# Pairing local kernels in one PSUM bank, holding a weight split back, and reordering two short tails in a decoder trunk

## The chip, the cores and the metric

The kernel runs on one core of one Trainium2 chip. The metric is the device time in microseconds (us); three runs of the kernel before gave 1273.04, 1273.29 and 1273.45 us, so 1273.29 us is its median. The five engines of the core are named as the profile names them: PE (matrix multiply; PEld is its weight load), DVE (vector), ACT (scalar and activation), POOL (GpSimd) and SP (which mostly issues DMAs). Each engine works through its own instructions in program order, and waits where one needs another engine's result.

## What is computed

Two layers with a width of 1024 over 256 tokens, in fp32. Each layer is a half-step SwiGLU feed-forward block (FFN), a mixer, a cross-attention into 256 memory tokens, and a second FFN, all with a residual add and an RMS norm in front. Layer 0 mixes with S5, a diagonal state-space model over 64 groups of 16 channels; layer 1 with RetNet retention. The end is one more RMS norm.

```python
def _rmsnorm(x, g):
    return x * lax.rsqrt(jnp.mean(x * x, axis=-1, keepdims=True) + EPS) * g

def reference(x, mem, ...):
    mem_n = _rmsnorm(mem, mem_norm)
    for i in range(DEPTH):
        g = norm_gains[i]
        x = x + 0.5 * _swiglu(_rmsnorm(x, g[0]), ffn1_w_in[i], ffn1_w_out[i])
        h = _rmsnorm(x, g[1])
        mix = _s5_mixer(h, ...) if i % 2 == 0 else _retention_mixer(h, positions, ...)
        x = x + mix
        x = x + _memory_cross_attention(_rmsnorm(x, g[2]), mem_n, ...)
        x = x + 0.5 * _swiglu(_rmsnorm(x, g[3]), ffn2_w_in[i], ffn2_w_out[i])
    return _rmsnorm(x, final_norm)

# S5: state x_t = a * x_{t-1} + Bbar u_t (complex, diagonal), then
y = gelu(real(C x_t) + d_skip * u);  a, gate = split(y @ w_glu);  mix = a * sigmoid(gate)
```

## The kernel before

**Precision and weights.** Every large product is made of three matmuls: both factors are split into a rounded part (`hi`) and the rest (`lo`), and hi·hi, hi·lo and lo·hi are summed in PSUM. `Stream` (`ws`, line 35) feeds the weights in the fixed order of `plan`: a DMA on SP's queue fills one of 5 `raw` buffers, ACT copies it to `wh` (line 87), DVE subtracts to `wl` (line 89, or line 106 where the subtraction was held and released), for at most 7 open pieces. Where in the program a split is issued is decided when the program is written out: `tick()` may split one piece, if a rough clock (`ws.t`) says that its DMA has landed, and `get()` forces the piece that is needed. `ws.limit` names the first piece in the plan that a tick must not split. A forced `get` does not look at it.

**Order.** The schedule is manual: engines run what the program text issues, in that order. `bg` is a list of background generators; the FFN and projection loops call `bg_step()` between their matmuls, and each call runs a generator to its next `yield`.

**The tables of S5** (`s5_tables`, line 576) are such a generator. It runs inside the first FFN, up to some 197 us. Its last loop goes over 8 index values `q` ("quarters" in the code). `vrev(q, part)` lets DVE make a reversed table in `Vr2`, which has two slots, `q % 2`; `vt(q, b)` transposes half of it on PE (4 transposes into a bank named `tp`), and ACT copies it out; `kernels(q)` (line 750) makes the local convolution kernel of 8 steps: 8 calls of `small` (matmuls with 32 columns of weights, 16 records in the trace), into 128 columns of a `tp` bank, one ACT copy to `pads`, and one short DVE operation that adds the skip term. `ca` makes another table on DVE.

**PSUM.** `acc()` takes one of 6 banks, `ptb()` one of 2. A pool gives out the bank that has been free the longest, counted along the program text. So which bank a tile gets depends on which tiles were released before it.

**The S5 input** (`S5In`, line 792; `s5`, line 824). After the first FFN the normalised input goes to DRAM (`xn_d`) and comes back re-laid as `xc`. Meanwhile `fill(us)` feeds PE with pieces of the memory's key and value projections: `kv_unit(0, u)` for units 0 to 5, 48 steps in all; one step is 6 matmuls of 128x256 for units 0 to 3 and of 128x512 for units 4 and 5. `fill(11.8)` (line 848) takes 19 steps: units 0 and 1 whole, each ending in a split of its bank by ACT (`kvh`) and DVE (`kvl`), and steps 0 to 2 of unit 2. Unit 2 has two weight pieces: `(("kv",0,2),0)` for steps 0 to 3 and `(("kv",0,2),1)` for steps 4 to 7. Then ACT and DVE copy `xc` to `xg`, two each in turn (line 852); PE transposes `xg` in 4 groups of 4 into the two `pt` banks, and ACT and DVE copy them to `U` (line 857); `fill(1.0)` takes steps 3 and 4 of unit 2; and the products `v` from `U` follow (line 868).

**The S5 output** (from line 938). After the scan over 32 chunk states (DVE, lines 887 to 890), `carry(q)` adds the carried state to the banks `ybank` with `small` matmuls; `gelu(0)` reads the banks of q 0 to 3 and `gelu(1)` those of q 4 to 7. `y_out(hf)` (line 942) transposes one time half of the result on PE, 2 times 4, into `pt` banks, and splits it into `yT` hi and lo. These splits have strided targets and are slow. `ws.hold()` keeps four subtractions of the output weights back until `ws.release()`, after the scan. `fill(1.3)` takes one step of unit 5. Then `glu_blocks` multiplies by the output weights, whose first block needs both halves: four matmuls with the weights that go with `y_out(0)`, then four with those of `y_out(1)`.

**The last norm** (`Final.stat`, line 1277) is called once per 128 tokens. The second call is the end of the program: ACT sums squares of both halves of the row (`mean_sq`, line 289), POOL adds them and EPS (line 282) and raises to -0.5 (line 283), DVE and ACT scale 512 columns each and each half goes out in its own DMA.

Of the kernel before, what the change touches and what calls it, by code (L numbers as in the profile page):

```python
# [10 lines left out]
F32 = mybir.dt.float32  # L11
# [3 lines left out]
AF = mybir.ActivationFunctionType  # L15
ALU = mybir.AluOpType
AX = mybir.AxisListType

P = 128
# [5 lines left out]
EPS = 1e-6  # L25
# [114 lines left out]
def tile_trunk(ctx: ExitStack, tc: tile.TileContext, I: dict, out: bass.AP):  # L140
    nc = tc.nc
    pe, act, dve, pool = nc.tensor, nc.scalar, nc.vector, nc.gpsimd
# [5 lines left out]
    sm = ctx.enter_context(tc.tile_pool(name="sm", bufs=2))  # L148
# [4 lines left out]
    def acc(name="acc"):  # L153
        return ps_acc.tile([P, 512], F32, tag="acc", name=name)

    def ptb(name="pt"):
        return ps_t.tile([P, 512], F32, tag="pt", name=name)
# [73 lines left out]
    ws = Stream(nc, raw_pool, w_pool, plan)  # L231
# [3 lines left out]
    neghalf = cpool.tile([P, 2], F32, tag="neghalf", name="neghalf")  # L235
    gT = cpool.tile([P, 72], F32, tag="gT", name="gT")
    x = big.tile([P, 2, D], F32, tag="x", name="x")
# [9 lines left out]
    def small(o, a, b, start, stop, at):  # L247
        ws.t += 0.074
        pe.matmul(o, lhsT=a, rhs=b, start=start, stop=stop, tile_position=at)  # L249
# [22 lines left out]
    rstd = {}  # L272
# [13 lines left out]
    def mean_sq(src, ss):  # L286

        junk = sm.tile([P, D], BF16, tag="junk", name="junk", bufs=1)
        act.activation(junk[:, 0:src.shape[-1]], src, AF.Square, scale=1.0 / 32.0, accum_out=ss)  # L289

    def ssq(src, parts=1):
        ss = sm.tile([P, 2], F32, tag="ss", name="ss", bufs=4)
        for i in range(parts):
            n = D // parts
            mean_sq(src[:, i * n:i * n + n], ss[:, i:i + 1])
        return rsqrt(ss[:, 0:1], 4, "rstd", ss[:, 1:2] if parts == 2 else None)
# [279 lines left out]
    def s5_tables():  # L576
# [15 lines left out]
        pt = ptb()  # L592
# [69 lines left out]
        for n in (1, 2, 4):  # L662
            t = [sm.tile([P, 4, 32], F32, tag="t512", name="tp", bufs=2)[:, 0:n] for _ in range(2)]
            a = [pw[:, c, n:n + 1].to_broadcast([P, n, 32]) for c in range(2)]
# [15 lines left out]
        t = [sm.tile([P, 32, 16], F32, tag="t512", name="tb", bufs=2) for _ in range(2)]  # L680
# [4 lines left out]
        E16 = sm.tile([P, 16], F32, tag="E16", name="E16", bufs=1)  # L685
        dve.tensor_reduce(E16, ident.rearrange("p (b h) -> p h b", h=16), axis=AX.X, op=ALU.add)
        dT = sm.tile([P, 8], F32, tag="dT", name="dT", bufs=1)
        pt = ptb()
# [6 lines left out]
        Cb = big.tile([P, 2, 32, 2, 16], F32, tag="W1", name="Cb")  # L695
        pool.memset(Cb.rearrange("p a b c d -> p (a b c d)"), 0.0)
        yield
        for c in range(2):
            for b in range(2):
                pt = acc("tp").rearrange("p (t r) -> p t r", t=4)  # L700
# [12 lines left out]
        Vr2 = big.tile([P, 2, 2, 4, 8, 16], F32, tag="Mh", name="Vr2")  # L713
# [27 lines left out]
        def vt(q, b):  # L741
            pt = acc("tp").rearrange("p (a e) -> p a e", a=4)
            for i in range(4):
                tr(pt[:, i], Vr2[:, q % 2, i % 2, 2 * b + i // 2].rearrange("p s h -> p (s h)"), ident)
            o = Yl[:, q] if q < 2 else sY[:, 0]
            act.copy(o[:, 512 * b:512 * b + 512], pt.rearrange("p a e -> p (a e)"))
            if b and q >= 2:
                pool.dma_start(out=tabV[q], in_=sY[:, 0])

        def kernels(q):  # L750
            Vr, pd = Vr2[:, q % 2], pads[q // 4][:, q % 4]
            pt = acc("tp")
            for c in range(2):
                for j in range(4):
                    small(pt[32 * j:32 * j + 32, 0:P], Cb[:, c, j * 8 + q].rearrange("p g h -> p (g h)"),
                          Vr[:, c, j].rearrange("p s h -> p (s h)"), c == 0, c == 1, (0, 32 * j))
            act.copy(pd, pt[:, 0:P].rearrange("p (s h) -> p s h", h=16))
            dve.scalar_tensor_tensor(out=pd[:, 7], in0=E16, scalar=dT[:, q:q + 1], in1=pd[:, 7], op0=ALU.mult, op1=ALU.add)

        for part in range(2):  # L760
            vrev(0, part)
            yield
        for q in range(8):
            vt(q, 0)
            if q < 7:
                vrev(q + 1, 0)
            yield
            vt(q, 1)
            kernels(q)
            if q < 7:  # L770
                vrev(q + 1, 1)
            yield
            for part in range(2):
                ca(q, part)
                yield
# [48 lines left out]
    def s5(si, kv, fill, nxt):  # L824
# [9 lines left out]
        def local_table(q):  # L834
# [6 lines left out]
            for b in range(2):  # L841
# [3 lines left out]
                    tr(pt[:, i], pd[:, 7 - t:15 - t].rearrange("p s h -> p (s h)"), ident)  # L845
                act.copy(lv[:, 4 * b:4 * b + 4], pt.rearrange("p t (g h) -> p t g h", h=16))

        fill(11.8)
        alt = [act.copy, dve.tensor_copy]
        xg = big.tile([P, 16, 8, 16], F32, tag="xTh", name="xg")  # L850
        for b in range(4):
            alt[b % 2](xg[:, 4 * b:4 * b + 4], si.xc[:, :, 64 * b:64 * b + 64].rearrange("p s (g h) -> p g s h", h=16))
        for b in range(4):
            pt = ptb().rearrange("p (g e) -> p g e", g=4)
            for i in range(4):
                tr(pt[:, i], xg[:, 4 * b + i].rearrange("p s h -> p (s h)"), ident.rearrange("p (t j c) -> p j t c", t=2, j=4))
            alt[b % 2](U[:, 4 * b:4 * b + 4], pt)
        fill(1.0)
        vc = big.tile([P, 8, 2, 2, 64], F32, tag="xTh", name="vc")
        for b in range(4):  # L860
            bank = acc("v").rearrange("p (q c g s) -> p q c g s", q=2, c=2, g=2)
            for ql in range(2):
                q = 2 * b + ql
                t = tv[q] if q < 4 else tab("tabV", q)
# [10 lines left out]
        for b in range(4):  # L875
            pt = ptb()
            for i in range(4):
                q, c = 2 * b + i // 2, i % 2
# [25 lines left out]
        for qh in range(2):  # L904
            for g in range(2):
                ybank[qh, g] = acc("y").rearrange("p (q e) -> p q e", q=4)
            for ql in range(4):
                q = 4 * qh + ql
# [33 lines left out]
        def y_out(hf):  # L942
            if not yT:
                yT.extend(big.tile([P, 8, SEQ], F32R, tag=t, name="yT") for t in ("Yh", "Yl"))
            for b in range(2):
                pt = ptb().rearrange("p (t e) -> p t e", t=4)
                for i in range(4):
                    tr(pt[:, i], yg[:, 4 * b + i, hf * P:hf * P + P], ident)
                src = pt.rearrange("p t (j c) -> p t j c", j=4)
                o = [t.rearrange("p (j a) (c t) -> p a t j c", a=2, t=8)[:, hf, 4 * b:4 * b + 4] for t in yT]  # L950
                split(o[0], o[1], src)
# [26 lines left out]
        ws.limit = ("glu", 1, 0)  # L978
        ws.release()
        fill(1.3)  # L980
        for q in range(4, 8):
            carry(q)
        gelu(1)
        y_out(0)
        fill(1.3)
        y_out(1)
        fill(99)
# [284 lines left out]
    class Final:  # L1272
# [3 lines left out]

        def stat(self, tt):
            y = big.tile([P, D], F32, tag=("Yh", "Yl")[tt], name="fin")
            r = ssq(x[:, tt, :], 1 + tt)
            dve.tensor_mul(y, x[:, tt, :], self.gb)  # L1280
            for h, q in enumerate((nc.sync, act)):
                w = slice(h * 512, h * 512 + 512)
                if h:
                    act.activation(y[:, w], y[:, w], AF.Copy, scale=r)
                else:
                    dve.tensor_scalar_mul(y[:, w], y[:, w], r)
                q.dma_start(out=out[0, tt * P:tt * P + P, w], in_=y[:, w])
# [22 lines left out]
    with tc.manual_schedule():  # L1310
# [10 lines left out]
        e = sm.tile([P, 1], F32, tag="xw", name="xw", bufs=1)  # L1321
# [16 lines left out]
        pt = ptb()  # L1338
# [79 lines left out]
        kv = new_kv()  # L1418
# [9 lines left out]
        def fill(us, keep=0):  # L1428
            while us > 0 and len(todo) > keep:
                todo.pop()  # L1430
                us -= next(g)
            return len(todo) > keep
# [58 lines left out]
```

## Time and profile before

| what | us |
|---|---|
| median of three runs | 1273.29 |
| the profiled execution, its own time | 1273.82 |
| its span, first to last instruction | 1272.0 |
| S5 tables, loop over q (first to last DVE operation) | 83 to 197 |
| S5 input: PE between `fill(11.8)` and the products `v` | 230 to 241 |
| S5 output: from `carry(0)` to the first matmul of the output weights | 287.8 to 300.2 |
| last matmul to the end of the span | 1264.4 to 1272.0 |

The profile's page covers one execution. Its timeline lists instructions in order of time; a row has the start in us from the span's start, the duration (of all instructions, where a row merges several, with their count behind an x), engine, line, operation, tiles written and read, and in brackets how long the engine had been idle and which engine released it. Matmuls overlap: a 128x512 matmul is listed with 0.39 us but a new one starts every 0.23 us; a 128x256 one with 0.28 us starts every 0.12 us. So on PE starts are compared with starts. A row of the view of stages has the stretch, its length, the busy time of PE, PEld, DVE, ACT and POOL with counts, the granted PE clock (1.00 is full), the share of DMA engines and GB/s.

### The profile page before, as it was taken

Reading aid. Unit: us, or ns where it says so; the run is one execution under the profiler, and the core shown is the slowest. Engines: PE = TensorE matmul, PEld = TensorE weight load, DVE = VectorE, ACT = ScalarE, POOL = GpSimd, SP = SyncE. Lnnn points to the kernel's source line nnn. Section 1 sums busy time; section 2 is a strip of 40 time slices with the busy share of each in tenths; the row PEclk is TensorE's granted clock in tenths of the full one; section 3 lists DMA queues with packets and bytes.
Section 4 is the critical chain, followed back from the end, with each engine's and each line's share of the span. In section 5 each row is a group of like instructions: output and inputs, shape, how many; then the busy total and the mean of one; then the engine's idle time right before and its main releaser. Section 6 shows DMA issues by size and latency. Waiting matters only on the chain.

```text
span 1272.0 us, 18171 instructions
## 1 busy us (share of the span) xinstructions
PE 1253.9 (99%) x6888; PEld 1054.9 (83%) x6888; DVE 821.0 (65%) x1144; ACT 630.1 (50%) x849; POOL 58.1 (5%) x114
## 2 busy tenths in 40 slices
PE   9999999899999999999999999999999999999997
PEld 6878888777898888888888888899888898888886
DVE  6889996497567665545655546687655646755543
ACT  6464544465455555444544435544544445644532
POOL 3110011000000000001000000001100000000000
PEclk9999999899999999999999999999999999999999
DMA  8956775675735756664766664653674734766560
GB/s 259 254 160 211 256 266 186 216 265 164 226 124 167 236 178 186 206 186 144 225 199 196 187 195 136 221 173 115 220 228 133 232 99 133 233 198 195 181 187 33
DMA packets 166599, 242.05 MB, mean 190 GB/s; under 512 B 10720, under 2 KB 130640, under 8 KB 165872
## 3 DMA queue, kind: packets, MB, share of 16 engines
q1 hardware_dynamic: 162400, 227.59, 56.6%
q0 software_dynamic: 3328, 12.23, 2.8%
q8 instruction: 54, 0.88, 0.3%
q10 hardware_dynamic: 784, 1.08, 0.2%
q14 instruction: 33, 0.27, 0.1%
HBM read 229.32 MB, written 11.53 MB: 189 GB/s over the span
## 4 chain that ended last, share of the span: by engine, by line
PE 78%; DVE 3%; ACT 1%; issue 1%; DMA 1%; POOL 0%; POOLq 0%; SPq 0%; ACTq 0%; DVEq 0%
PE acc L241 61%; PE kv L241 4%; PE qk L241 4%; PE pt L245 3%; PE q L241 2%; DVE wl L89 1%; PE s L241 1%; PE o L241 1%; PE rv L241 1%; DVE t L887 1%; DVE S L890 0%; PE rs L241 0%; DMA raw<-in_xattn_w_kv 0%; PE y L249 0%; DVE S L889 0%
## 5 line engine op out<-in xcount | busy, mean ns | idle before, releaser
L89 DVE TENSOR_TENSOR wl<-raw,wh 128x1024 fp32r<-128x1024 f32 x400 | 483.8, 1223 | 200.4 <-ACT wh L87 187.1
L87 ACT CAST wh<-raw 128x1024 fp32r<-128x1024 f32 x408 | 423.0, 1051 | 191.3 <-PE acc L241 147.0
L241 PE MATMUL acc<-wh,xTh 128*128 128x512 f32 x864 | 325.4, 396 | 0.9 <-ACT wh L87 0.8
L241 PE MATMUL acc<-wh,xTl 128*128 128x512 f32 x864 | 319.9, 391 | 0.1
L241 PE MATMUL acc<-wl,xTh 128*128 128x512 f32 x864 | 319.2, 389 | 0.4 <-DVE wl L106 0.2
L241 PEld LDWEIGHTS acc<-wh,xTh 128*128 128x128 f32 x864 | 161.9, 188 | 34.9 <-ACT wh L87 2.2
L241 PEld LDWEIGHTS acc<-wh,xTl 128*128 128x128 f32 x864 | 161.6, 188 | 34.5 <-DVE xTl L1362 0.5
L241 PEld LDWEIGHTS acc<-wl,xTh 128*128 128x128 f32 x864 | 162.3, 188 | 33.0 <-DVE wl L106 0.6
L241 PE MATMUL acc<-wh,hTh 128*128 128x512 f32 x352 | 138.8, 394 | 0.0
L241 PE MATMUL acc<-wh,hTl 128*128 128x512 f32 x352 | 137.2, 390 | 0.0
L241 PE MATMUL acc<-wl,hTh 128*128 128x512 f32 x352 | 137.0, 389 | 0.0
L465 ACT ACTIVATE s<-acc,rstd 128x256 f32<-128x256 f32 x88 | 41.7, 474 | 156.1 <-PE acc L241 156.0
L467 DVE SCALAR_TENSOR_TENSOR h<-acc,rstd,s 128x256 f32<-128x256 f32 x88 | 42.2, 480 | 92.2 <-ACT s L465 92.2
L241 PEld LDWEIGHTS acc<-wh,hTh 128*128 128x128 f32 x352 | 66.1, 188 | 14.1 <-issue 0.8
L241 PEld LDWEIGHTS acc<-wh,hTl 128*128 128x128 f32 x352 | 66.1, 188 | 13.9
L241 PEld LDWEIGHTS acc<-wl,hTh 128*128 128x128 f32 x352 | 66.1, 188 | 13.2
L289 ACT ACTIVATE junk<-x 128x512 bf16<-128x512 f32 (+1 forms) x27 | 20.8, 772 | 72.5 <-DVE x L368 70.6
L368 DVE SCALAR_TENSOR_TENSOR x<-acc,x 128x512 f32<-128x512 f32 x28 | 18.5, 687 | 39.1 <-PE acc L241 39.1
L280 POOL TENSOR_SCALAR ms<-ss 128x1 f32<-128x1 f32 x11 | 3.3, 298 | 821.9 <-ACT junk L289 821.7
L241 PE MATMUL acc<-wh,ryT 128*128 128x512 f32 x128 | 40.1, 390 | 0.0
L241 PE MATMUL acc<-wh,yT 128*128 128x512 f32 x128 | 37.5, 390 | 0.0
L241 PE MATMUL kv<-memh,wh 128*128 128x256 f32 x128 | 37.1, 290 | 0.0
(295 smaller groups left out, 1617.3 us busy)
## 6 DMA issues: line engine op xcount, KB each, us to landing
raw<-in_ffn_w_in SPq DMA_DIRECT2D x352, 256.0 KB, 4.3
raw<-in_ffn_w_out SPq DMA_DIRECT2D x88, 512.0 KB, 4.1
raw<-in_ret_w_in SPq DMA_DIRECT2D x48, 512.0 KB, 4.5
raw<-in_xattn_w_kv SPq DMA_DIRECT2D x32, 512.0 KB, 5.0
raw<-in_s_w_glu SPq DMA_DIRECT2D x32, 256.0 KB, 4.0
raw<-in_xattn_w_q SPq DMA_DIRECT2D x16, 512.0 KB, 4.7
raw<-in_xattn_w_o SPq DMA_DIRECT2D x16, 512.0 KB, 3.6
raw<-in_ret_w_out SPq DMA_DIRECT2D x16, 512.0 KB, 4.5
```

The costliest lines, as they stand in the source:

```text
L87: self.nc.scalar.copy(hi, raw)
L89: self.nc.vector.tensor_sub(lo, raw, hi.bitcast(F32))
L241: pe.matmul(o, lhsT=a, rhs=b, start=start, stop=stop)
L245: pe.transpose(o, a, i)
L280: pool.tensor_scalar_add(t, ms, EPS)
L289: act.activation(junk[:, 0:src.shape[-1]], src, AF.Square, scale=1.0 / 32.0, accum_out=ss)
L368: dve.scalar_tensor_tensor(out=o, in0=banks[tt][h], scalar=c, in1=o, op0=ALU.mult, op1=ALU.add)
L465: act.activation(s, bank[:, 0:256], AF.Silu, scale=r)
L467: dve.scalar_tensor_tensor(out=h, in0=bank[:, 256:512], scalar=r, in1=s, op0=ALU.mult, op1=ALU.mult)
L887: dve.tensor_mul(t0, Sq[:, n - 1], a8[:, 0])
```

## The change

It has four parts. **Pairs:** `kernels(q0)` makes the local kernels of q0 and q0 + 1 in one bank, one after the other, with one ACT copy of 256 columns and two short DVE operations; it is called for odd q only, behind `vt(q, 0)`, where each q had its own call behind `vt(q, 1)`. **Hold:** during `fill(11.8)` and the copies to `xg` ticks split nothing from the second piece of unit 2 on. **Output:** `y_out` takes its banks from the six `acc` banks, and `y_out(0)` comes before `carry(4)` to `carry(7)`. **End:** for the second half of the tokens EPS is added to the first sum of squares on POOL while the second is still to come, the second is added to it by an ACT operation on 128x1, and POOL only raises to -0.5; the gain multiplication is done in two halves; and the last scaling gives 608 columns to DVE and 416 to ACT (both calls).

```diff
-        def kernels(q):
-            Vr, pd = Vr2[:, q % 2], pads[q // 4][:, q % 4]
-            pt = acc("tp")
-            for c in range(2):
-                for j in range(4):
-                    small(pt[32 * j:32 * j + 32, 0:P], Cb[:, c, j * 8 + q].rearrange("p g h -> p (g h)"),
-                          Vr[:, c, j].rearrange("p s h -> p (s h)"), c == 0, c == 1, (0, 32 * j))
-            act.copy(pd, pt[:, 0:P].rearrange("p (s h) -> p s h", h=16))
-            dve.scalar_tensor_tensor(out=pd[:, 7], in0=E16, scalar=dT[:, q:q + 1], in1=pd[:, 7], op0=ALU.mult, op1=ALU.add)
+        def kernels(q0):
+
+            pt = acc("tp").rearrange("p (a s h) -> p a s h", a=4, h=16)
+            for q in (q0, q0 + 1):
+                for c in range(2):
+                    for j in range(4):
+                        small(pt[32 * j:32 * j + 32, q - q0], Cb[:, c, j * 8 + q].rearrange("p g h -> p (g h)"),
+                              Vr2[:, q % 2, c, j].rearrange("p s h -> p (s h)"), c == 0 and q == q0, c == 1 and q > q0, (0, 32 * j))
+            pd = pads[q0 // 4][:, q0 % 4:q0 % 4 + 2]
+            act.copy(pd, pt[:, 0:2])
+            for i in range(2):
+                dve.scalar_tensor_tensor(out=pd[:, i, 7], in0=E16, scalar=dT[:, q0 + i:q0 + i + 1], in1=pd[:, i, 7], op0=ALU.mult, op1=ALU.add)
...
         for q in range(8):
             vt(q, 0)
+            if q % 2:
+                kernels(q - 1)
             if q < 7:
                 vrev(q + 1, 0)
             yield
             vt(q, 1)
-            kernels(q)
             if q < 7:
                 vrev(q + 1, 1)
...
+        ws.limit = (("kv", 0, 2), 1)
         fill(11.8)
...
             alt[b % 2](xg[:, 4 * b:4 * b + 4], si.xc[:, :, 64 * b:64 * b + 64].rearrange("p s (g h) -> p g s h", h=16))
+        ws.limit = None
...
             for b in range(2):
-                pt = ptb().rearrange("p (t e) -> p t e", t=4)
+                pt = acc("yt").rearrange("p (t e) -> p t e", t=4)
...
         ws.release()
         fill(1.3)
+        y_out(0)
         for q in range(4, 8):
             carry(q)
         gelu(1)
-        y_out(0)
         fill(1.3)
         y_out(1)
...
-            r = ssq(x[:, tt, :], 1 + tt)
-            dve.tensor_mul(y, x[:, tt, :], self.gb)
-            for h, q in enumerate((nc.sync, act)):
-                w = slice(h * 512, h * 512 + 512)
+            if tt:
+                ss = sm.tile([P, 2], F32, tag="ss", name="ss", bufs=4)
+                pre, r = (sm.tile([P, 1], F32, tag=t, name=t, bufs=n) for t, n in (("ms", 4), ("rstd", 4)))
+                mean_sq(x[:, 1, 0:512], ss[:, 0:1])
+                pool.tensor_scalar_add(pre, ss[:, 0:1], EPS)
+                mean_sq(x[:, 1, 512:1024], ss[:, 1:2])
+                for h in range(2):
+                    w = slice(h * 512, h * 512 + 512)
+                    dve.tensor_mul(y[:, w], x[:, 1, w], self.gb[:, w])
+                act.activation(ss[:, 1:2], ss[:, 1:2], AF.Identity, bias=pre)
+                pool.tensor_tensor(r, ss[:, 1:2], neghalf[:, 0:1], op=ALU.pow)
+            else:
+                r = ssq(x[:, 0, :])
+                dve.tensor_mul(y, x[:, 0, :], self.gb)
+            for h, (w, q) in enumerate(((slice(0, 608), nc.sync), (slice(608, 1024), act))):
```

## The prediction

> **What bounds the kernel now.** I read the page first, then the view of waits for PE, then stages.
>
> ```profile
> PE 1253.9 (99%) x6888; PEld 1054.9 (83%) x6888; DVE 821.0 (65%) x1144; ACT 630.1 (50%) x849; POOL 58.1 (5%) x114
> ...
> PEclk9999999899999999999999999999999999999999
> ...
> PE pt L245 <- ACT xg L852: 4.1, 1, 4.1
> PE pt L245 <- DVE yT L329: 1.3, 2, 0.9
> ...
> 230.00:234.16 4.16, 0.03 (x2) 0.01 (x1) 1.51 (x2) 2.59 (x5) 0.00 (x0) 1.00 1.04 402
> 234.16:241.00 6.84, 6.27 (x28) 5.38 (x28) 2.96 (x6) 1.64 (x3) 0.00 (x0) 0.53 0.45 156
> ```
>
> PE is busy nearly always, so time comes only from PE's stalls, from PE's own work, and from the stretch behind its last matmul. The two longest stalls that I can do something with are the first of `xg`, 4.1 us, and those for `yT`, 1.3 us. The two stage rows show that the first costs more than its length: PE does nothing for 4.16 us, and in the 6.84 us behind it the granted clock is 0.53 instead of 1.00. The page's row of clock, in 40 slices, has its only dip there. All four parts touch PE's stalls, its work or the tail, so I go through them in order of time.
>
> **1. Pairs of kernels.** The multiplications stay; what goes is four changes of PE from transposes to narrow matmuls and back.
>
> ```profile
> 101.30 0.39 PE L241 MATMUL acc<-wh,xTl 128*128 128x512 f32 x1
> ...
> 102.20 0.39 PE L241 MATMUL acc<-wl,xTh 128*128 128x512 f32 x1
> ...
> 159.45 0.39 PE L241 MATMUL acc<-wh,hTl 128*128 128x512 f32 x1
> ...
> 160.21 0.64 PE L249 MATMUL tp<-Vr,Cb 128*32 128x128 f32 x16
> ...
> 161.12 0.39 PE L241 MATMUL acc<-wl,hTh 128*128 128x512 f32 x1
> ```
>
> The first two rows stand around four transposes alone and one wide matmul: 102.20 - 101.30 = 0.90 us. The other pair stands around the same with a kernel group: 1.67 us. A group costs 0.77 us. Its 16 records start within 0.64 - 0.27 = 0.37 us (the last lasts 0.27), 0.025 each, so 16 more in the same group cost 0.40. A pair costs 0.77 + 0.40 instead of 1.54: 0.37 saved, four times **1.5 us**. Ends: 0 if the 0.37 us of change-over is paid for each set of weights, and nothing is lost, since no instruction is added on PE.
>
> The new place: `kernels` at odd q now stands ahead of `vrev(q + 1, 0)`, whose third DVE operation overwrites the slot that `kernels` reads, so a wait of DVE for PE is added. DVE's subtractions for `wl` would queue behind it. It is hidden as long as DVE runs behind PE there:
>
> ```profile
> 189.68 0.23 DVE L758 SCALAR_TENSOR_TENSOR pads<-E,dT,pads 128x16 f32<-128x16 f32 x1 [1.10 <-ACT pads L757]
> ```
>
> This 1.10 us is the only stop for `pads` in the table stage, at q = 7, where no `vrev` follows; in the middle DVE reaches `pads` only after ACT is through. Without that cover each of the three waits (q = 1, 3, 5) would cost DVE under 1.2 us (a pair on PE), ahead of `wl` that PE needs some us later: PE loses nothing. I take 0. Fewer and longer ACT copies (four for eight) lie beside PE. The saving reaches the end only if the input of S5 also comes 1.5 us earlier; the wait in the last row (DVE follows PE there, through ACT) says that the chain behind it does. I take 1.5.
>
> **2. Hold.** The chain of the 4.1 us stall, engine by engine (ACT, DVE, PE, DMA issues with their times to landing):
>
> ```profile
> 231.57 1.04 ACT L87 CAST wh<-raw 128x1024 fp32r<-128x1024 f32 x1 [7.24 <-DMA raw<-in_xattn_w_kv]
> 232.52 1.07 ACT L328 CAST kvh<-kv 128x512 fp32r<-128x512 f32 x2
> 233.47 1.15 ACT L852 COPY xg<-xc 128x512 f32<-128x512 f32 x2
> 235.02 0.59 ACT L857 COPY U<-pt 128x512 f32<-128x512 f32 x1 [0.40 <-PE pt L245]
> ...
> 232.65 1.23 DVE L89 TENSOR_TENSOR wl<-raw,wh 128x1024 fp32r<-128x1024 f32 x1 [7.07 <-ACT wh L87]
> ...
> 234.99 0.75 DVE L852 COPY xg<-xc 128x512 f32<-128x512 f32 x2
> 236.68 0.69 DVE L857 COPY U<-pt 128x512 f32<-128x512 f32 x1 [0.94 <-PE pt L245]
> ...
> 229.75 0.28 PE L241 MATMUL kv<-memh,wl 128*128 128x256 f32 x1
> 234.16 0.82 PE L245 MATMUL pt<-ident,xg 128*128 128x128 f32 x4 [4.13 <-ACT xg L852]
> ...
> 241.03 1.21 PE L249 MATMUL v<-tabV,U 128*32 128x128 f32 x32
> ...
> 225.05 0.98 SPq L816 DMA_DIRECT2D xc<-xn_d  x2
> 226.38 0.39 SPq L69 DMA_DIRECT2D raw<-in_xattn_w_kv  x1
> ...
> xc<-xn_d SPq DMA_DIRECT2D x1, 256.0 KB, 3.8
> ...
> raw<-in_xattn_w_kv SPq DMA_DIRECT2D x1, 512.0 KB, 5.1
> ```
>
> ACT stands 7.24 us before a cast whose weights are issued at 226.38 and land 5.1 later, at 231.5. Behind that cast, in order, wait two finished `kvh` and the first `xg`. `xc` itself is there earlier: the second of its two issues starts near 225.7, plus 3.8 is 229.5. With the cast gone from this place the `kv` splits run when PE ends a unit, and `xg` starts at 229.6. In before's times:
>
> ACT's first `xg` ends at 230.25 (half of the 1.15 row, plus start-up), DVE's two by 230.35. PE's transposes start at 230.3. Four of them are done 0.7 later; ACT's copy to `U` takes 0.59, DVE's 0.69; there are two `pt` banks, so group 3 waits for ACT's copy (231.6) and group 4 for DVE's (232.2). PE is through the transposes at 232.65 and takes step 3, 6 matmuls at 0.12 us, to 233.4. The held cast comes behind it in the text, and on ACT behind the last `U`: 232.95 to 234.0; its subtraction on DVE, 1.22 us, to 235.25. Here is the **new wait**: step 4 needs both, and PE stands some 1.7 us for them, until 235.3. Queued behind on PE are only the rest of step 4 (0.5 us) and then `v`; on ACT and DVE nothing that PE needs sooner. `v` starts at 236.0, not 241.03: 5.0 us. On SP, the next weight DMA, which had its buffer from the subtraction at 233.9, gets it at 235.25 and lands near 240.4; its cast in the new timetable would start at 239.6, so ACT and DVE are up to 0.8 us late there, of which I let 0.1 through. Sum: **4.9 us**. Ends: 3.6 if all waits come 1.3 us worse (another subtraction's length), 5.3 if the 1.7 us wait is hidden in part. No transfer that PE's products wait for becomes later than PE, since all later buffers are freed by PE's own progress.
>
> This sum has the clock at 1.00; at most 0.47 x 6.84 = 3.2 us of it are the clock's.
>
> The Trainium skill, "TensorE: Matmul & The Clock Gate", Part 1, says that an idle window of about 3.4 us halves PE's clock and that a busy one of that length restores it. The trace agrees: 4.16 us idle, then 6.84 us at 0.53. Its Part 4 says that transposes do not count as busy for that gate. This speaks against the change, since its stretch from 230 to 236 is mostly transposes and short waits; the rival "half clock all the same", below, is what it would do here.
>
> **3. Output.** PE, then ACT:
>
> ```profile
> 291.67 1.31 PE L249 MATMUL y<-ytab,S 64*32 64x128 f32 x61
> ...
> 293.94 1.10 PE L245 MATMUL pt<-ident,yg 128*128 128x128 f32 x8
> ...
> 296.03 0.40 PE L241 MATMUL kv<-wh,meml 128*128 128x512 f32 x1
> 297.34 0.66 PE L245 MATMUL pt<-ident,yg 128*128 128x128 f32 x4 [0.91 <-DVE yT L329]
> 298.34 0.66 PE L245 MATMUL pt<-ident,yg 128*128 128x128 f32 x4 [0.34 <-DVE yT L329]
> 298.75 0.48 PE L241 MATMUL kv<-wh,memh 128*128 128x512 f32 x1
> ...
> 300.21 1.98 PE L241 MATMUL acc<-wh,yT 128*128 128x512 f32 x8
> ...
> 290.14 1.09 ACT L969 ACTIVATE yg<-y 128x512 f32<-128x512 f32 x2 [4.47 <-PE y L249]
> 298.03 2.17 ACT L328 CAST yT<-pt 128x512 fp32r<-128x512 f32 x2 [0.92 <-PE pt L245]
> ```
>
> `y_out(1)` waits for its two `pt` banks until DVE has split `y_out(0)`. With four more banks and `y_out(0)` earlier, its transposes can follow the matmul at 296.03 at once: 296.3 instead of 297.34. Eight take 0.85 (1.10 less the overlap of the last), so the next step starts at 297.15, not 298.75: **1.6 us**, and the output weights at 298.6, not 300.21. Three new waits, and why I cost them at nothing. `y_out(0)` now stands where `carry(4)` began, at 291.67, and needs `gelu(0)`, which ends at 290.14 + 1.09 = 291.23: 0.4 us to spare. `gelu(1)` waits on ACT behind the two casts of `y_out(0)` (2.2 us from 292.4, so until 294.6); `carry(7)` ends at 294.8, later. The fifth matmul of the output weights, at 299.5, needs both casts of `y_out(1)`: 296.3 + 0.7 + 2.17 = 299.2. That cover is 0.3 us; what is beyond it would be lost. Ends: 1.6 gained, 0.8 lost (rival "late bank").
>
> **4. End.** DVE, then POOL and ACT:
>
> ```profile
> 1265.53 1.23 DVE L1280 TENSOR_TENSOR fin<-x,fb 128x1024 f32<-128x1024 f32 x1
> ...
> 1266.41 0.52 POOL L282 TENSOR_SCALAR ms<-ss 128x1 f32<-128x1 f32 x1 [6.92 <-ACT junk L289]
> 1267.01 0.56 POOL L283 TENSOR_TENSOR rstd<-ms,neghalf 128x1 f32<-128x1 f32 x1
> 1267.60 0.72 ACT L1284 ACTIVATE fin<-fin,rstd 128x512 f32<-128x512 f32 x1 [1.29 <-POOL rstd L283]
> ...
> L1097 ACT ACTIVATE xw<-neghalf 128x1 f32<-128x1 f32 x2 | 0.4, 203 | 0.0
> ```
>
> POOL's addition, 1266.41 to 1266.93, is replaced by an ACT operation on 128x1; the nearest row has 203 ns, so the power could start at 1266.6, 0.4 earlier. DVE's gain multiplication still runs until 1266.8, and POOL's addition took 0.52 beside it, so I let the power run beside it too and end 0.2 earlier. ACT scales 416 columns for 512, 0.08 less (0.14 by proportion as the upper end). **0.3 us**; ends 0 and 0.5.
>
> The Trainium skill, "SBUF — State Buffer", section on who interferes with whom, says that a DVE instruction with two SBUF inputs and a POOL instruction that reads SBUF block each other for a whole instruction. By it the power would start at 1266.8 and the sum stays at 0.3; without it, 0.5. The addition that ended 0.17 us behind DVE's multiplication agrees.
>
> **Sum:** 1.5 + 4.9 + 1.6 + 0.3 = 8.3 us. The profiled execution took 1273.82 us (span 1272.0), so its like would take 1265.5. The median of the runs is 0.53 lower, 1273.29: **1265.0 us**.
>
> **Rivals.** *Half clock all the same* (12%): the gate closes in the thin stretch from 231 to 236 and PE runs the next 6.8 us at about half, as it does now. That doubles some 3 us of PE work, partly under the waits for `U`: 2.5 us lost, 1267.5. For it: PE would be busy little over half of that stretch. Against: no idle piece is over 1.7 us, and PE's other stalls, 1.3 us and less, leave no dip in the row of clock. *Pairs save nothing* (13%): 1266.5; against it stands that the 0.37 us were worked out from a group's two ends. *Late bank* (8%): the bank of the first output product is one that unit 5 gives back last; then it waits for DVE's split of `kv` behind both of `yT`, 296.3 + 4.1 + 0.7 = 301.1 against 300.21, so 1.6 gained becomes 0.8 lost, 1267.4. By the order of release in the text it gets a bank of `gelu(1)`. *The wait moves* (8%): the held piece costs PE 2 us more than I have, 1267.0. *The hold does not hold* (4%), another path splits the piece as before: 1269.9. *Slower* (3%): the clock falls at the S5 input and, in a stage of transposes and narrow matmuls, stays at half. Its price is half of its length; over 17 us it eats the 8.3, and from 22 us the kernel is slower by over 0.2%; through to the carries at 287 it would be some 1290 us. Against it: now the clock returns after 6.8 us in this very stage.
>
> **How the numbers follow.** The forecast, 1265.0, has 52%. Range 1263.8 to 1268.3: below, the good ends of parts 2 and 4 (0.6) and the 0.53 between one execution and the median; above, every rival but the last two, and two small misses together. A difference under 0.2%, 2.5 us, cannot be told from none. Faster by more, that is under 1270.8: 93%; the same, a sum of several misses, 4%; slower 3%.
>
> **What would show it.** In the profile after: PE's wait for `xg` under 0.5 us and the clock 1.00 from 230 to 241; a wait of 1 to 2 us of PE `kv` for `wl`; no wait of PE for `yT`, and the output weights 1.6 us sooner behind `carry(0)`; four groups of 32 narrow records; last matmul to span end 0.3 shorter. If the first two fail, the prediction is wrong by most of its size.

## The result and the profile after

| | before | after |
|---|---|---|
| median of four runs each, us | 1273.35 | 1266.32 |
| lowest to highest | 1273.04 to 1273.45 | 1266.27 to 1266.88 |
| ratio, with its 95% interval | | 0.9944 [0.9932, 0.9957] |
| the profiled execution's own time | 1273.82 | 1266.29 |
| its span | 1272.0 | 1264.5 |

The changed kernel is 0.56% faster. The forecast was 1265.0 us in a range of 1263.8 to 1268.3; the time lies inside, 1.3 us above the forecast.

First the stages. The view cuts the span into stretches that begin and end with the same PE instruction in both kernels: the first matmul of unit 0 of `kv`, the first `xg` transpose, the first `v`, the first `carry` matmul and the first one of the output weights. The columns are the stretch, its length, then busy time and count for PE, PEld, DVE, ACT and POOL, the granted clock of PE, and the DMA share with GB/s. Before:

```profile
216.19:234.16 17.97, 13.84 (x116) 13.63 (x114) 7.94 (x10) 5.09 (x10) 1.80 (x4) 1.00 0.68 205
234.16:241.03 6.87, 6.30 (x28) 5.38 (x29) 2.96 (x6) 1.64 (x3) 0.00 (x0) 0.53 0.45 156
241.03:287.83 46.80, 45.24 (x481) 36.79 (x480) 38.21 (x140) 27.81 (x39) 3.46 (x6) 1.00 0.70 237
287.83:300.21 12.38, 11.12 (x290) 9.14 (x291) 9.36 (x7) 6.37 (x9) 0.00 (x0) 1.00 0.66 211
```

After:

```profile
214.77:228.95 14.18, 13.84 (x115) 13.62 (x113) 8.34 (x12) 4.24 (x9) 1.80 (x4) 1.00 0.59 155
228.95:234.49 5.54, 4.17 (x29) 3.28 (x29) 2.75 (x4) 2.59 (x4) 0.00 (x0) 1.00 0.92 369
234.49:281.14 46.65, 45.12 (x481) 36.68 (x480) 38.18 (x140) 27.81 (x39) 3.45 (x6) 1.00 0.74 249
281.14:292.77 11.63, 10.91 (x291) 9.25 (x292) 8.60 (x7) 5.82 (x8) 0.00 (x0) 1.00 0.69 215
```

Then the end. Each block has first the stretch from the start of the last matmul to the end of the span, cut as above. The rows below it are from the timeline (start, duration, engine, line, operation, output and inputs, count, and in brackets the idle time of the engine before it with what ended that); the last is from the view of DMAs (KB and us from issue to landing) and is the write of ACT's columns. Before (the last scaling, from 1267.60, 0.72 long, is quoted in the prediction):

```profile
1264.38:1272.04 7.66, 0.39 (x2) 0.00 (x0) 2.40 (x3) 1.45 (x3) 1.08 (x2) 0.79 0.18 68
...
out<-fin ACTq DMA_DIRECT2D x1, 256.0 KB, 2.5
```

After:

```profile
1256.99:1264.51 7.52, 0.39 (x2) 0.00 (x0) 2.43 (x4) 1.66 (x4) 0.72 (x2) 0.72 0.18 70
...
1258.03 1.28 DVE L1293 TENSOR_TENSOR fin<-x,fb 128x512 f32<-128x512 f32 x2
...
1259.02 0.29 ACT L1294 ACTIVATE ss<-ss,ms 128x1 f32<-128x1 f32 x1
1259.40 0.57 POOL L1295 TENSOR_TENSOR rstd<-ss,neghalf 128x1 f32<-128x1 f32 x1 [2.25 <-ACT ss L1294]
1260.00 0.64 ACT L1301 ACTIVATE fin<-fin,rstd 128x416 f32<-128x416 f32 x1 [0.68 <-POOL rstd L1295]
...
out<-fin ACTq DMA_DIRECT2D x1, 208.0 KB, 2.6
```

Set side by side, in us, with the prediction's terms:

| stretch | before | after | difference | predicted |
|---|---|---|---|---|
| span's start to unit 0 of `kv` | 216.19 | 214.77 | -1.42 | -1.5 (pairs) |
| unit 0 of `kv` to `v` | 24.84 | 19.72 | -5.12 | -5.0 (hold) |
| `v` to the first `carry` | 46.80 | 46.65 | -0.15 | +0.1 |
| first `carry` to the output weights | 12.38 | 11.63 | **-0.75** | **-1.6** |
| output weights to the last matmul | 964.17 | 964.22 | +0.05 | 0 |
| last matmul's start to the last scaling's end | 3.94 | 3.65 | -0.29 | -0.3 |
| the last scaling's end to the end of the span | 3.72 | 3.87 | **+0.15** | 0 |

The pairs and the hold did what the sum says. The output stage gave less than half, and half of what the end won up to the last scaling is lost again behind it. The rows sum to 7.53 us for 8.3.

**The S5 input after**, from the timeline, ACT, DVE, PE:

```profile
228.28 1.14 ACT L857 COPY xg<-xc 128x512 f32<-128x512 f32 x2 [1.21 <-DMA xc<-xn_d]
...
231.46 1.05 ACT L87 CAST wh<-raw 128x1024 fp32r<-128x1024 f32 x1
...
232.54 1.22 DVE L89 TENSOR_TENSOR wl<-raw,wh 128x1024 fp32r<-128x1024 f32 x1 [0.33 <-ACT wh L87]
...
228.95 1.09 PE L245 MATMUL pt<-ident,xg 128*128 128x128 f32 x8 [0.35 <-ACT xg L857]
230.28 1.20 PE L245 MATMUL pt<-ident,xg 128*128 128x128 f32 x8 [0.24 <-ACT U L863]
...
232.56 0.39 PE L241 MATMUL kv<-memh,wh 128*128 128x256 f32 x1 [0.36 <-ACT wh L87]
...
233.82 0.39 PE L241 MATMUL kv<-memh,wl 128*128 128x256 f32 x1 [0.76 <-DVE wl L89]
```

The copy to `xg` is released by its own data, `xc`, and no longer stands behind the weights' cast. PE's wait for it is 0.35 us instead of 4.13, and the clock is 1.00 in both stretches. The cast and the subtraction that were held back run behind the copies to `U`, and PE waits for them at step 4, 0.36 + 0.76 = 1.12 us. The prediction had 1.7 us for this new wait.

**The output stage after**, from the timeline, ACT, then PE:

```profile
287.29 2.19 ACT L328 CAST yT<-yt 128x512 fp32r<-128x512 f32 x2 [2.76 <-issue]
289.22 1.16 ACT L975 ACTIVATE yg<-y 128x512 f32<-128x512 f32 x2
...
284.86 1.03 PE L245 MATMUL yt<-ident,yg 128*128 128x128 f32 x8
285.82 1.29 PE L249 MATMUL y<-ytab,S 64*32 64x128 f32 x60
...
290.44 1.09 PE L245 MATMUL yt<-ident,yg 128*128 128x128 f32 x8 [0.72 <-ACT yg L975]
```

PE waits for no bank any more, as predicted. But it stands 0.72 us for `yg`, the result of `gelu(1)`. That activation starts at 289.22, behind two casts of `y_out(0)`. The first cast needs only the first four of the eight transposes; even the last of them was done at 284.86 + 1.03 = 285.89, yet the casts start at 287.29, and ACT has nothing to do for 2.76 us before them. "issue" means that the trace names no releaser. What ends just then, with a few more records behind the 60 shown, is the `ytab` matmuls, those of `carry(4)` and `carry(5)`.

**Theory.** `y_out` puts the high half of `yT` into the buffer with the tag `Yh`. That buffer holds the tables `tC[4]` and `tC[5]` (`ytab`), which `carry(4)` and `carry(5)` still read. In the kernel before, `y_out(0)` came behind the carries, so it made no difference. Moved ahead of them, its casts wait for two carries that follow it, `gelu(1)` queues behind the casts on ACT, and PE waits for `gelu(1)`. **Rivals:** the casts wait for a bank or for something that the hold delays; or the extra banks are worth less than the prediction has.

### The profile page after: what moved, and what is told of

Read it like the earlier page. It is cut to its first block, busy times and chain, and to the rows that moved or that the text cites. A ratio compares the mean times of both kernels' runs of the same rounds, so it can differ in the third digit from the quotient of the medians.

```text
span 1264.5 us, 18176 instructions
## 1 busy us (share of the span) xinstructions
PE 1249.1 (99%) x6888; PEld 1052.5 (83%) x6888; DVE 820.8 (65%) x1145; ACT 630.4 (50%) x846; POOL 58.9 (5%) x114
## 4 chain that ended last, share of the span: by engine, by line
PE 77%; DVE 3%; issue 1%; ACT 1%; POOLq 0%; POOL 0%
PE acc L241 62%; PE kv L241 4%; PE qk L241 4%; PE pt L245 3%; PE q L241 2%; PE s L241 1%; PE o L241 1%; DVE wl L89 1%; PE rv L241 1%; DVE t L893 1%; DVE S L896 1%; PE rs L241 0%; DVE S L895 0%; DVE t L894 0%; PE v L249 0%
## 5 line engine op out<-in xcount | busy, mean ns | idle before, releaser
L241 PE MATMUL kv<-memh,wl 128*128 128x256 f32 x128 | 36.3, 284 | 0.8 <-DVE wl L89 0.8
```

What stands on the lines that cost most here:

```text
L241: pe.matmul(o, lhsT=a, rhs=b, start=start, stop=stop)
```

## The experiments

By the first transposes of the S5 tables the clock times of two executions already differ by up to 1.7 us (68.56 us in e4, 70.28 in e2), so lengths between two instructions of one execution are compared. The first four kernels ran beside twenty runs of the kernel before (median 1273.57 us), the others beside nine (1273.04). The changed kernel was not run again beside them. The ratio is to the kernel before, with its 95% interval.

| kernel | from | median, us | ratio |
|---|---|---|---|
| e1_group_two_banks | before | 1272.25 | 0.9992 [0.9983, 1.0001] |
| e2_hold_only | before | 1268.88 | 0.9962 [0.9948, 0.9976] |
| e3_warm_stall | before | 1271.43 | 0.9983 [0.9974, 0.9993] |
| e4_out_old_order | after | 1265.34 | 0.9934 [0.9919, 0.9949] |
| e5_yT_in_W1 | after | 1265.55 | 0.9937 [0.9924, 0.9949] |
| e6_step4_behind_v | after | 1265.24 | 0.9936 [0.9923, 0.9948] |
| e7_both | after | 1264.42 | 0.9930 [0.9917, 0.9944] |
| e8_both_W1 | after | 1264.98 | 0.9932 [0.9920, 0.9945] |

### Pairs: is it the grouping or the bank?

```diff
             vt(q, 0)
+            if q % 2:
+                kernels(q - 1)
+                kernels(q)
...
             vt(q, 1)
-            kernels(q)
```

> The kernel before, with only the place of the kernel groups changed: at odd q the groups of q - 1 and q are issued one behind the other, each still in a bank of its own with its own ACT copy. Theory (PE pays 0.37 us for each change between transposes, narrow and wide matmuls, so four changes fewer save 1.4 to 1.5 us): the first matmul of the memory projection (216.19 us in the kernel before, 214.77 in the changed one) starts at 214.8, and the time falls by 1.4 us to about 1271.9 us. Rival (the shared bank and the one copy for two bring the gain): that matmul starts within 0.4 us of 216.2 and the time stays at 1273.

The timeline of this kernel, an early and a late pair on PE, and the weight load in the middle of the late one:

```profile
101.89 1.08 PE L249 MATMUL tp<-Vr,Cb 128*32 128x128 f32 x32
...
156.21 1.43 PE L249 MATMUL tp<-Vr,Cb 128*32 128x128 f32 x32
...
156.99 0.38 PEld L249 LDWEIGHTS tp<-Vr,Cb 128*32 128x32 f32 x16 [0.41 <-ACT sY L746]
```

The first `kv` matmul starts at 216.09 us, where the rival has it, and not at 214.8; but the rows tell why. In the first two pairs 32 records take 1.08 us, as in the changed kernel: grouping by itself saves the change-over. In the last two a pair takes 1.43: the second group waits 0.41 us for a bank that ACT is still copying to `sY`. From the first table transposes to unit 0 of `kv` this kernel gains 0.64 us, the change 1.39, and 2 x 0.35 of the difference of 0.75 are these two waits. So the time comes from the grouping, and the one bank keeps it from being lost again in half of the pairs. At the first `carry` the gain is 1.42 all the same: the stall of `xg` and the slow stretch behind it, which this kernel still has, are 0.65 shorter (17.97 + 6.87 before, 17.69 + 6.50 here), and the rest lies behind `v`. Why they shrink was not tried; where the half clock falls has a part in it (last section). As a time the gain, 1.3 us, is not told from none.

### The hold alone, and the clock alone

```diff
+        ws.limit = (("kv", 0, 2), 1)
         fill(11.8)
...
+        ws.limit = None
```

> The kernel before with only the hold during the first fill and the copies to xg. Theory (the cast in front of the copies is the whole cause of the stall and of the half clock): from the first matmul of the memory projection to the first product v there are 24.84 us in the kernel before and 19.72 in the changed one; here 19.7, with the clock at 1.00, and about 5.1 us less in all, 1268.2 us. Rival (the changed kernel kept its clock because the pairs had moved this stretch against the clock's own windows): some rows at half clock, and a gain of 2 to 3.5 us, about 1270 to 1271.

Its stages, `kv` unit 0 to 234.16, then on until `v` is nearly over:

```profile
217.58:234.16 16.58, 15.81 (x130) 15.24 (x129) 9.18 (x13) 5.48 (x11) 1.80 (x4) 1.00 0.62 189
234.16:241.00 6.84, 5.72 (x143) 5.08 (x141) 2.61 (x3) 2.56 (x5) 0.00 (x0) 1.00 0.66 239
```

The clock is 1.00 where the kernel before had 0.53, and `v` begins 19.90 us behind unit 0 of `kv` (24.84 before, 19.72 in the changed kernel). The two lines alone carry 4.94 of the 5.12 us. The median, 1268.88 us, is 4.7 us under the kernel before, nearer to the theory than to the rival.

How much of it is the clock's? The next kernel keeps the stall and fills PE's idle time with 33 matmuls whose result nobody reads:

```diff
+    mem_t = []
...
         fill(11.8)
+        warm = acc("warm")
+        for _ in range(33):
+            pe.matmul(warm[:, 0:256], lhsT=mem_t[0].hi[:, 0, 0:P], rhs=mem_t[0].hi[:, 0], start=True, stop=True)
...
-        mem_t = []
```

> The kernel before with 33 more matmuls of 128x256 on PE, into a spare bank that nothing reads, between the first fill and the transposes of xg; they take about 4.0 us, the length of the stall, so the stall stays but PE is not idle in it. Theory (the half clock comes from PE's idleness and costs up to 3.2 us by itself): the first copy to xg still starts near 233.5 us, the clock stays at 1.00, and v starts 2 to 3 us sooner, at 238 to 239 for 241.03; time about 1270.5 to 1271.3. Rival (the 6.84 us behind the stall are slow for another reason, such as the transfers that run beside it): v starts at 241 or later and the time is 1273.3 or more.

Its stages, cut as in the first view:

```profile
216.37:234.73 18.36, 17.79 (x149) 17.59 (x147) 7.93 (x10) 5.09 (x10) 1.80 (x4) 1.00 0.67 211
234.73:239.55 4.82, 3.73 (x28) 3.16 (x29) 2.96 (x6) 1.64 (x3) 0.00 (x0) 1.00 0.54 184
```

`xg` starts no earlier (0.39 later, as the weight's cast in front of its copies does), yet the clock is 1.00 and the stretch from `xg` to `v` takes 4.82 us for 6.87. The first copy starts 0.68 us ahead of PE's first transpose, 0.69 before, so the two stretches can be compared. PE's idleness is what halved the clock, and the half clock cost 2.05 us up to `v`; the prediction had it at 3.2 at most. From unit 0 of `kv` to `v` the gain is 1.66 us, under the 2 to 3 expected, since `xg` came later; the median, 1271.43 us, is 0.1 above the expected range and well under the rival's 1273.3. The term of 5.12 us then reads: 4.13 - 0.35 = 3.78 of the stall, 2.05 of the clock, less 1.12 of the new waits, and 0.41 for the transposes: without waits for the weight the stretch has 5.54 - 1.12 = 4.42 us after and 4.82 here, where the copies to `xg` come late for PE.

### Output: order, or buffer?

First the old place of `y_out(0)`, with the new banks:

```diff
         fill(1.3)
-        y_out(0)
         for q in range(4, 8):
             carry(q)
         gelu(1)
+        y_out(0)
         fill(1.3)
```

> The changed kernel with y_out(0) put back behind the carries and gelu(1), its banks still from the six. Theory (yT lies in the buffer from which carry(4) and carry(5) still read their table, so with y_out(0) ahead of them ACT's casts wait for carry(5), gelu(1) waits behind the casts, and PE for gelu(1)): no wait of PE for yg; from the first carry to the first matmul of the output weights 10.8 us, where the changed kernel has 11.63 and the one before 12.38; time 0.7 to 0.8 us under the changed kernel, about 1265.6. Rival (ACT's wait of 2.76 us in front of the casts is one for the subtractions that were held, or for the banks): the casts wait as before, and the stretch stays at 11.6 or becomes longer; 1266.3 to 1267.

ACT in the timeline of this kernel:

```profile
287.02 1.09 ACT L975 ACTIVATE yg<-y 128x512 f32<-128x512 f32 x2 [2.76 <-PE y L249]
287.99 4.21 ACT L328 CAST yT<-yt 128x512 fp32r<-128x512 f32 x4
```

`gelu(1)` is released by PE, at the end of the carries, and four casts follow without a gap. From the first `carry` (280.85) to the output weights (291.54) it takes 10.69 us: 1.69 less than before, which is the term that the prediction had. So the banks give all of it, and the new order takes more than half of it back. Its median is 0.98 us under the change's, but it doesn't tell which thing the early casts wait for. The next one does: the order of the change stays, and one word moves `yT` to the buffer that held `U`, which is read for the last time before the carries.

```diff
-                yT.extend(big.tile([P, 8, SEQ], F32R, tag=t, name="yT") for t in ("Yh", "Yl"))
+                yT.extend(big.tile([P, 8, SEQ], F32R, tag=t, name="yT") for t in ("W1", "Yl"))
```

> The changed kernel with one word changed: the high half of yT lies in the buffer that held U (W1) instead of the buffer of the tables tC[4] and tC[5] (Yh). The order with y_out(0) ahead of carry(4) stays. Theory (ACT's casts of y_out(0) wait until carry(4) and carry(5) have read the buffer, and gelu(1) stands behind them): the first cast starts about 4.5 us behind the first carry matmul instead of 6.15, the activations of gelu(1) start as soon as carry(7) is done, PE waits for no yg, the first output-weight matmul comes 10.7 us behind the first carry instead of 11.63, and the time is 0.7 to 1.0 us under the changed kernel, near 1265.4 us. Rival (the casts wait for something else, such as a bank or the held subtractions): the casts stay at 6.1 us behind the first carry and the time stays at 1266.3 us.

ACT in the timeline:

```profile
285.51 2.78 ACT L328 CAST yT<-yt 128x512 fp32r<-128x512 f32 x2 [0.96 <-PE yt L245]
288.19 1.09 ACT L975 ACTIVATE yg<-y 128x512 f32<-128x512 f32 x2
```

The first cast is now released by its transposes, 285.51 - 281.07 = 4.44 us behind the first `carry` instead of 6.15, and the output weights come 10.81 us behind it (11.63 in the change). The held subtractions still run on DVE until 287.53 here, 2 us behind that start, and the banks are those of the change. The buffer was the wait; the rivals fall. `gelu(1)`, at 288.19, is still behind the casts but early enough, since PE is in `kv` matmuls until its transposes of `y_out(1)` start, at 289.62.

### The waits that the hold leaves

```diff
-        fill(1.0)
+        fill(0.6)
         vc = big.tile([P, 8, 2, 2, 64], F32, tag="xTh", name="vc")
...
-        fill(1.0)
+        fill(1.9)
```

> The changed kernel with the wide loop's step 4 of the memory projection put behind v instead of ahead of it: ahead of v runs step 3 alone, behind v steps 4 to 6. In the changed kernel PE waited 0.36 us for the cast and 0.76 us for the low half of the weight that is held back, both ahead of v. Theory (these two waits are the price that the hold leaves): v starts right behind the transposes of xg and step 3, both waits are gone, and the time is about 1.1 us under the changed kernel, near 1265.2 us. Rival (the table tabV or the bank copies end last at v, or the same 1.1 us comes back as idle time between v and vc): the gain is under 0.4 us, 1265.9 us or more.

PE in the timeline of this kernel, then three rows of its waits (total, times, longest):

```profile
230.49 1.20 PE L245 MATMUL pt<-ident,xg 128*128 128x128 f32 x8 [0.24 <-ACT U L863]
...
232.34 1.08 PE L249 MATMUL v<-tabV,U 128*32 128x128 f32 x32
...
PE kv L241 <- DVE kvl L329: 0.9, 1, 0.9
...
PE pt L245 <- DVE S L886: 0.7, 2, 0.4
...
PE pt L245 <- ACT S L886: 0.2, 1, 0.2
```

The same waits in the changed kernel:

```profile
PE kv L241 <- DVE kvl L329: 0.6, 1, 0.6
...
PE pt L245 <- ACT S L886: 0.4, 2, 0.2
```

`v` starts right behind step 3, 17.39 us behind unit 0 of `kv` instead of 19.72, and both waits for the held weight are gone. The median is 1.1 us under the change, as the theory has it. The trace gives it less: 0.8 at the output weights, because a part comes back as waits later: 0.9 us for `kvl` where the change has 0.6, and 0.9 for the copies to `S` where it has 0.4. Between 0.8 and 1.1 these five runs don't decide.

### Together

e7 takes the old place of `y_out(0)` and the later step 4, e8 the buffer `W1` and the later step 4.

> The changed kernel with two edits: y_out(0) stands behind the carries and gelu(1) again, as in the kernel before (its own banks stay), and step 4 of the memory projection stands behind v. Theory: the two stretches are apart in time (220 to 240 us and 281 to 293 us), so the gains add: 1.0 us from the first edit, which was measured alone at 1265.34 us, and 1.1 us from the second, in all near 1264.2 us. Rival (the second edit is worth nothing): 1265.3 us.

> The changed kernel with two edits: the high half of yT in the buffer W1, with y_out(0) still ahead of carry(4), and step 4 of the memory projection behind v. Theory: the gains add, 0.7 to 1.0 us and 1.1 us, so 1264.2 to 1264.5 us; if moving y_out(0) forward is worth anything once its buffer is free, this is under the kernel with y_out(0) behind the carries, and if not, the two are the same within 0.3 us.

e7 in stages, `kv` unit 0, `xg`, `v`, first `carry`, output weights:

```profile
214.64:229.11 14.47, 13.84 (x116) 13.63 (x114) 8.40 (x12) 4.24 (x9) 1.80 (x4) 1.00 0.58 157
229.11:232.28 3.17, 2.93 (x23) 2.44 (x23) 1.44 (x3) 2.20 (x4) 0.00 (x0) 1.00 1.01 403
232.28:280.07 47.79, 45.83 (x488) 37.40 (x487) 39.38 (x142) 28.42 (x40) 3.45 (x6) 1.00 0.75 257
280.07:290.74 10.67, 10.67 (x290) 9.21 (x291) 8.61 (x7) 5.61 (x8) 0.00 (x0) 1.00 0.64 205
```

In the last stretch PE is busy for its whole length, 10.67 of 10.67: no wait is left there. From unit 0 of `kv` to the output weights e7 takes 76.10 us, the change 78.00, the kernel before 84.02: the two gains add. e8 takes 76.08. With its buffer free, `y_out(0)` ahead of the carries is worth nothing more than behind them; the stages of e7 and e8 are equal within 0.02 us. Their medians are 0.56 us apart, more than the 0.3 expected, and e8's lies 0.5 above its expected range; of the 0.38 us between the two profiled executions, 0.36 lie ahead of these stages (unit 0 of `kv` starts at 215.00 in e8, 214.64 in e7). At 1264.42 us e7 is the fastest kernel here, 0.70% under the kernel before; its interval overlaps that of the change, and that it is faster than the change rests on the medians (1.9 us) and on the stages (1.9 us) together.

## Why the prediction was right, and where it was not

**Pairs, 1.5 predicted, 1.42 measured** (1.39 counted from the first transposes of the tables). The change-over worked out from one group's two ends holds: 32 records take 1.08 us, and the table stage lost nothing to the moved `kernels`. The rival "pairs save nothing" falls. What the prediction did not see is that the one bank is needed: with a bank each, the late pairs wait.

**Hold, 4.9 predicted, 5.12 to `v` and 0.15 more behind it measured.** The mechanism is the predicted one, step for step: the `xg` copy released by `xc`, the clock at 1.00, a new wait for the held weight. Its timetable holds within 0.1 us at each step: counted from unit 0 of `kv`, `v` was put at 19.81 and comes at 19.72. The new wait reads 1.12 us for 1.7 because two matmuls of step 4 run between its two halves, not because anything came sooner. Behind `v`, 0.1 us was to be lost and 0.15 was won: in the kernel before, the end of the half clock reaches into the `v` matmuls, whose first 32 take 1.21 us for 1.08 after. The sum had no term for that. The rival "half clock all the same" falls: PE's longest idle piece in that stretch is 0.76 us. The rule of the Trainium skill ("TensorE: Matmul & The Clock Gate", Part 4) by which transposes don't count as busy was not put to the test in this stretch: between the last `kv` matmul before `xg` (228.33 + 0.28) and step 3 (231.24) lie 2.6 us of transposes and waits, less than the window of about 3.4 us in Part 1. Another stretch does test it (last section).

**Output, 1.6 predicted, 0.75 measured. This is the step that failed:** "`gelu(1)` waits on ACT behind the two casts of `y_out(0)` (2.2 us from 292.4, so until 294.6)". The 292.4 let the casts start as soon as the first transposes are done. They start 1.8 us after that (2.43 us behind the first transposes, 0.63 in e5), since their target buffer is still being read by the carries that the change puts behind them. The prediction counted the new order's banks and engine queues, but not whose data lies in the buffer that the moved step writes. With these 1.8 us, `gelu(1)` is late. The other half of the term, that PE's wait was one for banks and that the transposes then follow at once, is shown right by e4: 1.69 us.

**End, 0.3 predicted, 0.29 measured up to the last scaling, but 0.14 to the end of the span** (7.66 and 7.52 us; 7.65 in e1, which has the old end, 7.51 in e7), in the trace alone; the runs can't tell 0.3 us. The prediction's sign, 0.3 less from the last matmul to the end of the span, did not come: its term stops at the scaling and puts what follows at no change. Behind the scaling the writes land later, ACT's 208 KB 2.6 us after issue where 256 KB took 2.5, SP's 304 KB 2.3 where 256 KB took 2.0. Which of the uneven split and the shorter distance between the two issues (0.11 us for 0.24) does it, no run tells. The ACT operation took 0.29 us, not the 0.20 of the nearest row. What the Trainium skill says of DVE and POOL ("SBUF — State Buffer", section on who interferes with whom) was not tested: DVE's multiplication ends at 1259.31 and the ACT operation at 1259.31 too, so POOL's start at 1259.40 answers to either.

**From the sum to the time.** The rows of the table give 7.53 us, 0.77 under the sum: 0.85 from the output stage and 0.16 from the end, less 0.37 that the hold gave beyond its term, and 0.13 of small differences. The profiled executions are as far apart, 1273.82 - 1266.29 = 7.53. The other 0.5 us of the miss is the 0.53 that was taken off because before's profiled execution lay above its median; after's lies 0.03 under its own.

## What to carry over

When a step is moved forward, look up which buffer it writes and who reads that buffer last, in the new order; a free engine and a free bank are not enough, and what queues behind the step on its engine pays too. When a long PE stall is removed, price the clock with it: here 2.05 us of 5.1. Where a weight is held back, move the step that needs it as well, or the wait only moves.

## What was not expected

The clock's return in the kernel before can be read by the microsecond (columns as in the first view):

```profile
233.00:234.00 1.00, 0.00 (x0) 0.00 (x0) 1.00 (x2) 1.00 (x4) 0.00 (x0) 1.00 1.04 418
234.00:235.00 1.00, 0.82 (x4) 0.43 (x4) 1.00 (x3) 0.62 (x2) 0.00 (x0) 0.75 1.04 418
...
241.00:242.00 1.00, 1.00 (x33) 0.95 (x36) 0.00 (x0) 0.00 (x0) 0.00 (x0) 0.83 0.00 0
```

A mean of 0.75 means that it fell near 234.5, when PE had already begun again, and 0.83 that it came back near 241.3, so the half clock lasted 6.8 us. That is twice the busy window of about 3.4 us that the Trainium skill ("TensorE: Matmul & The Clock Gate", Part 1) gives for the return. The timeline of PE tells what it did in them:

```profile
235.55 2.99 PE L245 MATMUL pt<-ident,xg 128*128 128x128 f32 x12 [0.57 <-DVE xg L852]
238.19 0.56 PE L241 MATMUL kv<-memh,wh 128*128 128x256 f32 x1
```

The first 3.7 us, until 238.19, were transposes with waits between them, the other 3.1 matmuls. This fits the rule of the Trainium skill ("TensorE: Matmul & The Clock Gate", Part 4) that transposes don't count, and it fits as well that the first half had idle pieces; for the return no run here tells the two apart.

In e1 the half clock lasts 6.8 us as well, but it begins near 232.9 (mean 0.97 from 232 to 233), in the stall, and is over near 239.8 (0.61 from 239 to 240), ahead of `v`. PE works under it for 6.0 us instead of 6.8. So what such a stall costs depends also on where it lies against the clock's changes.

For keeping the full clock a run does tell. In e6 PE has nothing but transposes and waits for 3.98 us, and the clock stays at 1.00. The second row is e6's clock at its end, the third that of the kernel before:

```profile
238.39:242.37 3.98, 3.04 (x24) 2.33 (x23) 2.50 (x4) 1.96 (x4) 0.00 (x0) 1.00 0.89 282
...
1259.00:1260.00 1.00, 0.00 (x0) 0.00 (x0) 0.54 (x1) 0.64 (x1) 0.31 (x1) 0.62 0.00 0
...
1268.00:1269.00 1.00, 0.00 (x0) 0.00 (x0) 0.09 (x1) 0.33 (x1) 0.00 (x0) 0.87 0.05 14
```

By these means the clock of the kernel before changes near 234.50, 241.34 and 1268.74, which lie 2 and 301 times 3.413 us apart. If e6's changes keep to such a grid, its fall near 1259.24 puts a whole window from 238.7 to 242.1, inside the transposes. If transposes did not count, the clock would have fallen there, as it did in the stall. So in this kernel they kept it up, against that rule of the Trainium skill, on which the prediction in part rested its rival "half clock all the same".

One POOL addition of 128x1, line 282, took 0.52 us in before's last norm, beside DVE's multiplication; the median of its nine calls is 0.30 (least, median and most in ns). No run takes DVE away from it.

```profile
L282 POOL TENSOR_SCALAR ms<-ss x9: 302/303/516, 24.7 to 1266.4; 128x1 f32<-128x1 f32 x9
```
